# The causal mask of a forgetting-attention stage, carried by two copies of the gate row

## The chip, the cores and the metric

The kernel runs on one core of one Trainium2 chip. The metric is the device time of one execution in microseconds (us), lower is better; the kernel before takes 1213.95 us (median of 3 runs, 1213.93 to 1214.04). A core has TensorE (PE in the profile, its weight loads PEld), VectorE (DVE), ScalarE (ACT), GpSimd (POOL) and SyncE (SP), each with its own instruction stream, and 16 DMA engines that move data between HBM and on-chip memory. Transfers can be issued from SP, ACT and POOL.

## The reference: what is computed

One decoder layer on a sequence of S = 1024 rows of width D = 1024, in float32. The part that matters here is the forgetting attention (FoX): 8 heads of width 64, with a causal softmax whose scores carry the difference of two cumulative sums of log forget gates:

```python
cum = jnp.cumsum(log_f, axis=1).transpose(0, 2, 1)          # (B, heads, S)
s = jnp.einsum('bhqd,bhkd->bhqk', qi, kh) * scale
s = s + ci[..., None] - cum[:, :, None, :]
s = jnp.where(key_pos[None, :] <= q_pos[:, None], s, -jnp.inf)
p = jax.nn.softmax(s, axis=-1)
out = jnp.einsum('bhqk,bhkd->bhqd', p, vh)
```

Around it stand a retention group of 4 heads of width 128, the output projection, a layer norm, an up projection to 2 x 2816 channels with a convolution of width 3, GELU times gate, a down projection and a second layer norm.

## The kernel before

Float32 products are made of three products of split operands (high with high, high with low, low with high), so that every value has a "hi" and a "lo" tile. The kernel has four stages in time: projections and retention (a block of its own, lines 208 to 745, whose order a scheduler sets from a simulated timeline), the FoX stage (its loop stands at lines 1173 to 1226), the output projection, and the channel mixer. The change touches the end of the first block and the FoX stage.

**The FoX loop** runs over 64 steps, `s_ = 8h + i`: head h, block i of 128 queries. A step does the following.
- `fox_scores` (L783): TensorE multiplies the queries of block i with the keys 0 to 128(i+1), two products per cut (L799 with the high part of q, L800 with the low part), into a two-bank PSUM tile `ps` (two buffers). The signs are such that a masked place must become large, so TensorE then adds the mask: a bfloat16 identity times a bfloat16 triangle of 1e30 (`identb`, `maskb`, L803) into the diagonal block. DVE adds the gate row `nb` (the cumulative gates of the head, the same in all 128 partitions) and takes the minimum of each row in one pass (L805). ScalarE takes the exponential and its sum (L812), DVE the reciprocal (L815), POOL multiplies (L816).
- three steps later, `fox_turn` (L849) transposes the probabilities on TensorE (L866) and splits them: ScalarE writes the high part (L874), DVE the low part (L875). At three steps of each head `fox_pv` (L877) multiplies them with the values (L886); ScalarE copies one half of the result into `mixF` (L899), and DVE adds the other half at once (L900).
- `fox_proj` (L757) projects q and k of this head (second half of the sequence, at i < 3) and of the next one (i >= 3): 3 products of 128x512 for each of 8 pieces of the weights (L765, L766, L767). ScalarE and DVE then write `qh`, `ks`, `ql` (L771 to L781).
- `fox_w(h + 2)` at i = 4 loads the weights `wqkr` of the head after next on SP and splits them: one ScalarE copy of 128x1024 (L641), two DVE subtractions of 128x512 (L644). Each head has its own pair of weight tiles.
- `fox_alloc` (L750) at i = 3 takes the next head's tiles and loads its `nb`, 512 KB, on SP (L753), from `cum_d` in HBM. That array is written once, at the end of the first block: `cum_forget` (L709, two small products and a copy), `cum_store` (L719, a transposition, a copy, and the store L725), in the last two of 16 steps of the value projection.
- beside this, work for later stages is threaded in: the output weights are split (`park_load` L1028, `park_high` L1032, `park_low` L1039, `park_store` L1045, `wod<-park`), read back in the last head (`wo_load`, L1051), and base values for the down projection are copied in HBM (`down_base`, L1154, `td<-in_w_down_dram`, 44 copies of 256 KB at i = 6 of each head). All these issue on SP.

**Order.** Outside the first block the instructions are written in the order of the loop, and the framework moves some of them (transfers above all). Each engine then runs its stream in order and waits at semaphores. SP and ACT transfers share a set of completion semaphores, which they take in rotation. Tiles come from pools with a fixed number of 4 KB buffers (16 with tag X, 10 with tag VM); a load waits until the last reader of the buffer is done.

## Time and profile before

| what | us |
|---|---|
| median of 3 runs | 1213.95 |
| the profiled execution: its own time | 1213.8 |
| its span, first to last instruction | 1212.1 |
| TensorE busy over the span | 1195.2 |
| FoX stage in the span | 268 to 490 |
| TensorE busy in the FoX stage | 219.09 of 222 |
| one head of the FoX stage | about 25.7 |

The granted TensorE clock was 0.998 of full speed on average. A row of a timeline gives the start, the duration, engine, line, operation, output and inputs, shape and count, and, in brackets, the idle time of the engine just before it with what ended it. Matmuls are pipelined: their durations overlap, so the pace is read from the distance of their starts. A row of a group gives the count, the busy time in us, the mean of one in ns, and the idle time before. A row of the waits gives who waited for whom: us in total, times, longest us.

### The profile page before, as it was taken

What the parts mean: (1) busy time and instruction counts of PE and PEld (TensorE: products, weight loads), DVE (VectorE), ACT (ScalarE), POOL (GpSimd) and SP (SyncE); (2) the same over time, 40 slices, a digit from 0 to 9 for tenths busy, and PEclk for the clock granted to TensorE, in tenths of its full rate; (3) what the DMA queues carried; (4) which work ended last, traced back from release to release, by engine and by line L of the source; (5) the groups of instructions that cost most, each with busy time, mean ns of one, the idle gap of its engine ahead of it and who ended that gap; (6) DMA issues with size and microseconds to landing.
All of it is one profiled execution on the core that took longest, in us unless ns stands there. A gap on an engine that the chain in (4) does not pass through costs nothing.

```text
span 1212.1 us, 17100 instructions
## 1 busy us (share of the span) xinstructions
PE 1195.2 (99%) x5957; PEld 1000.4 (83%) x5957; DVE 912.2 (75%) x1749; ACT 655.7 (54%) x1209; POOL 229.6 (19%) x274
## 2 busy tenths in 40 slices
PE   8999999999999999999999999999999999999997
PEld 6788888997888888888888888888888888888885
DVE  7847657766888888456988778787787875886686
ACT  6635445346777776567754545454454555644452
POOL 0015345012333333000021322211000010000021
PEclk9999999999999999999999999999999999999999
DMA  9524354605474659223268987776554589975741
GB/s 359 227 87 121 134 158 138 202 34 175 160 239 156 191 162 356 94 79 113 87 181 203 205 210 182 176 180 175 155 139 125 145 238 289 326 247 190 263 175 70
DMA packets 94279, 216.57 MB, mean 179 GB/s; under 512 B 10784, under 2 KB 17136, under 8 KB 94192
## 3 DMA queue, kind: packets, MB, share of 16 engines
q1 hardware_dynamic: 81520, 192.40, 45.7%
q0 software_dynamic: 12672, 23.07, 11.9%
q8 instruction: 47, 0.77, 0.3%
q14 instruction: 40, 0.33, 0.1%
HBM read 173.45 MB, written 76.59 MB: 206 GB/s over the span
## 4 chain that ended last, share of the span: by engine, by line
PE 91%; DMA 4%; DVE 2%; ACT 1%; issue 0%; SPq 0%; DVEq 0%
PE rp L152 11%; PE dX L1531 10%; PE dZ L1531 7%; PE uX L1306 7%; PE uX L1307 7%; PE uX L1305 7%; PE uY L1307 5%; PE uY L1306 5%; PE uY L1305 5%; PE vp L152 4%; PE pv L886 3%; DMA ada<-in_ada_dram 3%; PE op L191 2%; PE op L189 2%; PE op L190 2%; PE pt L866 2%
## 5 line engine op out<-in xcount | busy, mean ns | idle before, releaser
L152 PE MATMUL rp<-wr,hhi 128*128 128x512 f32 x400 | 127.9, 401 | 0.0
L1517 DVE TENSOR_TENSOR dl<-dr,dh 128x1024 fp32r<-128x1024 f32 x66 | 80.5, 1238 | 33.8 <-ACT dh L1505 31.5
L816 POOL TENSOR_TENSOR S<-S,dn 128x128 f32<-128x128 f32 (+3 forms) x64 | 74.2, 1166 | 151.3 <-DVE dn L815 112.0
L1505 ACT CAST dh<-dr 128x1024 fp32r<-128x1024 f32 x58 | 59.8, 1051 | 65.6 <-DMA dr<-td 30.3
L1148 POOL DMA_DIRECT2D sd<-gd x22 | 18.1, 823 | 396.9 <-DMA sd<-y 226.2
L152 PEld LDWEIGHTS rp<-wr,hhi 128*128 128x128 f32 x400 | 71.6, 189 | 12.7
L152 PE MATMUL rp<-wr,hlo 128*128 128x512 f32 x200 | 78.6, 393 | 0.0
L1531 PE MATMUL dX<-dl,dh 128*128 128x512 f32 x176 | 68.5, 389 | 0.0
L1531 PE MATMUL dX<-dh,dl 128*128 128x512 f32 x176 | 68.5, 389 | 0.0
L1531 PE MATMUL dX<-dh 128*128 128x512 f32 x176 | 68.5, 389 | 0.0
L1320 ACT COPY u<-uX 128x512 f32<-128x512 f32 x44 | 25.8, 586 | 70.3 <-PE uX L1307 70.3
L812 ACT ACTIVATE S<-S,mn 128x128 f32<-128x128 f32 (+3 forms) x64 | 49.8, 779 | 23.9 <-DVE mn L805 23.7
L152 DVE CUSTOM_DVE_ANT_0 ada<-ada,csb,bcol 128x1024 f32<-128x1024 f32 x46 | 60.1, 1310 | 3.4 <-DMA ada<-in_ada_dram 3.3
L875 DVE TENSOR_TENSOR pt<-pt,pt 128x384 fp32r<-128x384 f32 (+3 forms) x104 | 51.9, 517 | 10.2 <-ACT pt L874 9.8
L874 ACT CAST pt<-pt 128x384 fp32r<-128x384 f32 (+3 forms) x104 | 45.2, 454 | 24.9 <-PE pt L866 23.5
L765 PE MATMUL qk<-hhi,wqh 128*128 128x512 f32 x128 | 54.3, 424 | 1.8 <-DVE ks L777 1.5
L1531 PE MATMUL dZ<-dh 128*128 128x512 f32 x132 | 51.6, 391 | 0.0
L1531 PE MATMUL dZ<-dl,dh 128*128 128x512 f32 x132 | 51.4, 389 | 0.0
L1531 PE MATMUL dZ<-dh,dl 128*128 128x512 f32 x132 | 51.4, 389 | 0.0
L767 PE MATMUL qk<-hhi,wql 128*128 128x512 f32 x128 | 51.0, 399 | 0.0
L766 PE MATMUL qk<-hlo,wqh 128*128 128x512 f32 x128 | 50.9, 397 | 0.0
L189 PE MATMUL op<-wo,mxs 128*128 128x512 f32 x128 | 50.7, 396 | 0.0
(1049 smaller groups left out, 3653.3 us busy)
## 6 DMA issues: line engine op xcount, KB each, us to landing
ada<-in_ada_dram SPq DMA_DIRECT2D x48, 512.0 KB, 3.9
td<-in_w_down_dram SPq DMA_DIRECT2D x44, 256.0 KB, 5.6
wa<-in_w_up_dram SPq DMA_DIRECT2D x22, 512.0 KB, 4.5
wb<-in_w_up_dram SPq DMA_DIRECT2D x22, 512.0 KB, 3.7
gd<-y SPq DMA_DIRECT2D x22, 512.0 KB, 2.7
sd<-y SPq DMA_DIRECT2D x44, 256.0 KB, 3.1
dr<-sd SPq DMA_DIRECT2D x44, 256.0 KB, 4.2
dr<-td SPq DMA_DIRECT2D x44, 256.0 KB, 4.4
```

The costliest lines, as they stand in the source:

```text
L152: order[key] = fn(*args, **kw)
L189: mm(pt, ahi, whi, start=start, stop=False)
L765: nc.tensor.matmul(pt, whi[:, j, :], hhi[j][:, sl], start=(j == 0), stop=False)
L767: nc.tensor.matmul(pt, wlo[:, j, :], hhi[j][:, sl], start=False, stop=(j == ND - 1))
L816: nc.gpsimd.tensor_tensor(out=Ssb[:, :span], in0=Ssb[:, :span], in1=den.to_broadcast([P, span]), op=ALU.mult,)
L875: nc.vector.tensor_tensor(out=dl, in0=src, in1=f(dh), op=ALU.subtract)
L1305: nc.tensor.matmul(pt, whi, bh, start=start, stop=False, skip_group_check=True)
L1306: nc.tensor.matmul(pt, whi, bl, start=False, stop=False, skip_group_check=True)
L1307: nc.tensor.matmul(pt, wlo, bh, start=False, stop=stop, skip_group_check=True)
L1505: nc.scalar.copy(hi, raw)
L1517: nc.vector.tensor_tensor(out=lo, in0=raw, in1=f(hi), op=ALU.subtract)
L1531: nc.tensor.matmul(pt, w_[:, 0, q], m_[:, 1, :], start=start and n_ == 0, stop=stop and n_ == 2, skip_group_check=True)
```

## The change

Line numbers of the changed kernel are given as "new L...".

- The bfloat16 mask and identity, and the product that adds them to the scores, are gone. The triangle is a float32 tile on chip.
- Each head has two copies of its gate row, `nb[0]` and `nb[1]`, loaded at i = 3 of the head before (two loads of 512 KB on SP, new L640). Two steps later, `nb_mask` adds the triangle into every second block of them: into blocks 0, 2, 4, 6 of copy 0 and 1, 3, 5, 7 of copy 1, by one accumulating transfer per copy on POOL's queue (new L645, 128 x 4 x 128).
- Step i reads copy i modulo 2, whose block i carries the mask. Behind the exponential of the step, ScalarE issues a transfer that writes block i of that copy anew from `cum_d` (new L833, 128x128, 64 KB in rows of 512 bytes), for i < 6. The minimum of step i + 2 reads that block and waits for it.
- There is one pair of weight tiles `wqh`, `wql` for all heads. The raw weights of head h + 2 are loaded at i = 6, and the split is made in four pieces of 128x256 at steps 0 to 3 of the head before, behind the last product that reads the piece of the old weights.
- The DVE additions into `mixF` are written behind the step's transpositions and their copies (new L1227) and no longer straight behind the ScalarE copy.
- The cumulative gates are made and stored two steps earlier in the value projection (steps 12 and 13), the raw weights of head 1 and the gate row of head 0 are loaded at step 14, and head 0's mask is added at step 15.

The lines between the hunks are as before; the last hunks give the calls.

```diff
 ...
     ident = cp.tile([P, P], F32, tag="ident", name="ident")
-    identb = cp.tile([P, P], BF16, tag="identb", name="identb")
-    nc.vector.tensor_copy(identb, ident)
-    maskb = cp.tile([P, P], BF16, tag="maskb", name="maskb")
-    nc.gpsimd.memset(maskb, 0.0)
+    mask = cp.tile([P, P], F32, tag="mask", name="mask")
+    nc.gpsimd.memset(mask, 0.0)
     nc.gpsimd.affine_select(
-        out=maskb, in_=maskb, pattern=[[-1, P]], compare_op=ALU.is_ge,
+        out=mask, in_=mask, pattern=[[-1, P]], compare_op=ALU.is_ge,
         fill=BIG, base=0, channel_multiplier=1,
     )
 ...
-    def fox_w(h):
-        raw = slot("R", [P, ND, P], F32, f"wqkr{h}")
-        nc.sync.dma_start(raw, w_qk[h])
-        whi = slot("X", [P, ND, P], F32R, f"wqh{h}")
-        wlo = slot("X", [P, ND, P], F32R, f"wql{h}")
-        nc.scalar.copy(whi, raw)
-        for q in range(2):
-            sl = slice(4 * q, 4 * q + 4)
-            nc.vector.tensor_tensor(
-                out=wlo[:, sl, :], in0=raw[:, sl, :], in1=f(whi[:, sl, :]), op=ALU.subtract
-            )
-        return whi, wlo
+    wraw, nbs, pins = {}, {}, {}
+
+    def nb_load(h):
+        nbs[h] = []
+        for p in range(2):
+            nb = slot("X" if h < 2 or p == 0 else "VM", [P, S], F32, f"nb{h}_{p}")
+            pins["nb"] = nc.sync.dma_start(nb, cum_rows(h, 0, S))
+            nbs[h].append(nb)
+
+    def nb_mask(h):
+        for p in range(2):
+            nc.gpsimd.dma_start(
+                nbs[h][p].rearrange("p (k t q) -> p k t q", t=2, q=P)[:, :, p, :],
+                mask.unsqueeze(1).to_broadcast([P, NT // 2, P]),
+                accum_op=ALU.add, max_dma_last_dim=2048)
+
+    def cum_rows(h, k0, k1):
+        return bass.AP(tensor=cum_d.tensor, offset=cum_d.offset + h * S + k0,
+                       ap=[[0, P], [1, k1 - k0]])
+
+    def fox_load(h):
+        wraw[h] = slot("R", [P, ND, P], F32, f"wqkr{h}")
+        nc.sync.dma_start(wraw[h], w_qk[h])
+
+    def fox_w(h, part):
+        sl = slice(2 * part, 2 * part + 2)
+        raw, (whi, wlo) = wraw[h], wqk
+        nc.scalar.copy(whi[:, sl, :], raw[:, sl, :])
+        nc.vector.tensor_tensor(
+            out=wlo[:, sl, :], in0=raw[:, sl, :], in1=f(whi[:, sl, :]), op=ALU.subtract
+        )
 ...
         if q == 3:
-            w = fox_w(0)
+            wqk = [slot("X", [P, ND, P], F32R, f"wq{n}") for n in "hl"]
+            fox_load(0)
+            for part in range(4):
+                fox_w(0, part)
         if q == 8:
             Lp = log_forget()
+        if q == 12:
+            cum = cum_forget(Lp)
+        if q == 13:
+            cum_store(cum)
         if q == 14:
-            cum = cum_forget(Lp)
-            nw = fox_w(1)
+            fox_load(1)
+            nb_load(0)
         if q == 15:
-            cum_store(cum)
+            nb_mask(0)
     blk.__exit__(None, None, None)
     mixF = {}
-    pins = {}
     def fox_alloc(h):
         t = {n: slot("X", [P, S], F32R, f"{n}{h}") for n in ("qh", "ql", "ks")}
-        t["nb"] = slot("X" if h < 2 else "VM", [P, S], F32, f"nb{h}")
-        pins["nb"] = nc.sync.dma_start(t["nb"], bass.AP(
-            tensor=cum_d.tensor, offset=cum_d.offset + h * S, ap=[[0, P], [1, S]]))
+        t["nb"] = nbs[h]
         return t
-    def fox_proj(h, w, T, t, part):
-        whi, wlo = w
+
+    def fox_proj(h, T, t, part):
+        whi, wlo = wqk
         qh, ql, ks = T["qh"], T["ql"], T["ks"]
         sl = slice(t * 512, (t + 1) * 512)
         if part == 0:
 ...
             nc.vector.tensor_copy(ql[64:, sl], f(ql[:64, sl]))
     def fox_scores(h, i, T, beside=None):
-        qh, ql, ks, nb = T["qh"], T["ql"], T["ks"], T["nb"]
+        qh, ql, ks, nb = T["qh"], T["ql"], T["ks"], T["nb"][i % 2]
         span = (i + 1) * P
         tag = "S" if i % 2 == 0 else "R" if h < FH - 1 else "VM"
         Ssb = slot(tag, [P, S], F32, f"S{h}_{i}")
 ...
         qs = slice(i * P, (i + 1) * P)
         pt = bank2(f"ps{h}_{i}")[:, off:]
         for k0, k1 in cuts:
-            last = k0 <= i * P < k1
             nc.tensor.matmul(pt[:, k0:k1], qh[:, qs], ks[:, k0:k1], start=True, stop=False)
-            nc.tensor.matmul(pt[:, k0:k1], ql[:, qs], ks[:, k0:k1],
-                             start=False, stop=not last)
-            if last:
-                nc.tensor.matmul(pt[:, i * P:(i + 1) * P], identb, maskb,
-                                 start=False, stop=True)
+            nc.tensor.matmul(pt[:, k0:k1], ql[:, qs], ks[:, k0:k1], start=False, stop=True)
         pins["min"] = nc.vector.tensor_tensor_reduce(
             out=Ssb[:, :span], in0=pt[:, :span], in1=nb[:, :span], scale=1.0, scalar=3e38,
             op0=ALU.add, op1=ALU.min, accum_out=mn,
 ...
         pins["exp"] = nc.scalar.activation(
             Ssb[:, :span], Ssb[:, :span], AF.Exp, scale=-1.0, bias=mn, accum_out=den,
         )
+        if i + 2 < NT:
+            nc.scalar.dma_start(nb[:, qs], cum_rows(h, i * P, (i + 1) * P))
         nc.vector.reciprocal(den, den)
         nc.gpsimd.tensor_tensor(
             out=Ssb[:, :span], in0=Ssb[:, :span], in1=den.to_broadcast([P, span]),
 ...
                     skip_group_check=True,
                 )
         a, b = (0, 64) if not odd else (64, 0)
+        sums = []
         for j0, j1 in ((i0, min(i1, NT // 2 - 1)), (max(i0, NT // 2), i1)):
             if j0 > j1:
                 continue
 ...
             dst = mixF[h // 4, j0 // 4][a:a + 64, (h // 2) % 2, q0:q0 + (j1 + 1 - j0) * P]
             src = pv[:, (j0 - i0) * P:(j1 + 1 - i0) * P]
             nc.scalar.copy(dst, src[b:b + 64])
-            nc.vector.tensor_tensor(out=dst, in0=src[a:a + 64], in1=dst, op=ALU.add)
+            sums.append(dict(out=dst, in0=src[a:a + 64], in1=dst, op=ALU.add))
+        return sums
     AB = cp.tile([P, 2, ND], F32, tag="AB", name="AB")
 ...
     LOADS = {0: (4, 5), 1: (6, 7), 2: (0, 1), 3: (2, 3)}
     T = {0: fox_alloc(0)}
     for part in range(4):
-        fox_proj(0, w, T[0], 0, part)
-    fox_proj(0, w, T[0], 1, 0)
+        fox_proj(0, T[0], 0, part)
+    fox_proj(0, T[0], 1, 0)
     Sb = {}
     def proj(h, i):
         if i < 3:
-            fox_proj(h, w, T[h], 1, i + 1)
+            fox_proj(h, T[h], 1, i + 1)
         elif h + 1 < FH:
-            fox_proj(h + 1, w, T[h + 1], *divmod(i - 3, 4))
+            fox_proj(h + 1, T[h + 1], *divmod(i - 3, 4))
     for s_ in range(FH * NT + LAG + 1):
         h, i = divmod(s_, NT)
 ...
                     for half in range(2):
                         mixF[h // 4, half] = slot("VM", [P, 2, 512], F32, f"mixF{h // 4}_{half}")
             if i == 3:
-                w = nw
                 if h + 1 < FH:
+                    nb_load(h + 1)
                     T[h + 1] = fox_alloc(h + 1)
             if i >= 3:
                 proj(h, i)
             k = LOWS.get(s_)
             Sb[s_] = fox_scores(h, i, T[h], None if k is None else lambda: park_low(k))
-            if i == 4 and h + 2 < FH:
-                nw = fox_w(h + 2)
             if i == 6:
                 down_base(h)
             if k is not None:
 ...
                     with tc.issue_after(pins["exp"].ins):
                         park_high(k)
         r = s_ - LAG - 1
+        sums = []
         if r >= 0 and r % NT in (2, 5, 7):
-            fox_pv(r // NT, GROUP[r % NT])
+            sums = fox_pv(r // NT, GROUP[r % NT])
         r = s_ - LAG
         if 0 <= r < FH * NT:
             fox_turn(r // NT, r % NT, Sb.pop(r))
+        for kw in sums:
+            nc.vector.tensor_tensor(**kw)
         if h < FH and not (i >= 3):
             proj(h, i)
+        if i < 4 and h + 1 < FH:
+            fox_w(h + 1, i)
+        if i == 5 and h + 1 < FH:
+            nb_mask(h + 1)
+        if i == 6 and h + 2 < FH:
+            fox_load(h + 2)
         if h == FH - 1 and i == 0:
             for q in range(2):
                 op_load(q)
```

How the rows of the engines' streams move is shown at three places of head 2. In the names the first number is the head and the second the step or the part, the last one a buffer's own number; `hhi`, `hlo` are the two parts of the modulated input, `pt` the transposed probabilities, `S` the scores after the gates, `mn` and `dn` the row minimum and the sum.

TensorE, from the scores of step 5 to the transpositions of step 2 and the projection of head 3, before:

```order
L799 MATMUL ps2_5_3981<-ks2_3561,qh2_3559 128x256
L800 MATMUL ps2_5_3981<-ks2_3561,ql2_3560 128x256
L803 LDWEIGHTS identb_71
L803 MATMUL ps2_5_3981<-maskb_77,identb_71 128x128
L866 MATMUL pt2_2_0_3995<-ident_66,S2_2_3848 128x128 x3
L765 MATMUL qk3_0_3890<-hhi6_374,wqh3_3634 128x512
```

and in the changed kernel:

```order
L820 MATMUL ps2_5_3996<-ks2_3578,qh2_3576 128x256
L821 MATMUL ps2_5_3996<-ks2_3578,ql2_3577 128x256
L885 MATMUL pt2_2_0_4010<-ident_66,S2_2_3864 128x128 x3
L787 MATMUL qk3_0_3910<-hhi6_372,wqh_2584 128x512
L788 MATMUL qk3_0_3910<-hlo6_425,wqh_2584 128x512
```

The weight load and the product with the mask are gone between the second product of the scores and the transpositions; 64 such pairs leave the stream. Behind the 64 masks stand transpositions 26 times, products of a projection 17 times, products with the values 19 times, and scores twice. The changed stream has four more places where a product follows transpositions.

ScalarE, from the exponential of step 0 on, before:

```order
L812 ACTIVATE S2_0_3762,dn2_0_3769<-S2_0_3762,mn2_0_3763 128x128
L812 ACTIVATE S2_1_3791,dn2_1_3798<-S2_1_3791,mn2_1_3792 128x256
L1032 CAST park4_0_3748<-park4_1_3749 128x512
L899 COPY mixF0_0_3186<-pv1_1_3806 64x128
L874 CAST pt1_2_0_0_3823<-pt1_6_0_3829 128x4x128
L899 COPY mixF0_1_3187<-pv1_1_3806 64x256
L874 CAST pt1_2_1_0_3825<-pt1_6_1_3836 128x3x128
L874 CAST pt1_2_0_0_3823<-pt1_7_0_3859 128x4x128
L812 ACTIVATE S2_2_3848,dn2_2_3855<-S2_2_3848,mn2_2_3849 128x384
```

and in the changed kernel:

```order
L829 ACTIVATE S2_0_3774,dn2_0_3780<-S2_0_3774,mn2_0_3775 128x128
L833 DMA nb2_0_3572<-cum_d_2396 128x128
L661 CAST wqh_2584<-wqkr3_3739 128x256
L829 ACTIVATE S2_1_3805,dn2_1_3811<-S2_1_3805,mn2_1_3806 128x256
L833 DMA nb2_1_3574<-cum_d_2396 128x128
L1053 CAST park4_0_3760<-park4_1_3761 128x512
L919 COPY mixF0_0_3188<-pv1_1_3820 64x128
L919 COPY mixF0_1_3189<-pv1_1_3820 64x256
L893 CAST pt1_2_0_0_3835<-pt1_6_0_3841 128x4x128
L893 CAST pt1_2_1_0_3837<-pt1_6_1_3848 128x3x128
L661 CAST wqh_2584<-wqkr3_3739 128x256
L893 CAST pt1_2_0_0_3835<-pt1_7_0_3875 128x4x128
```

A transfer stands behind each exponential, ahead of the copies of `park`, `mixF` and `pt`, and the weight copies of 256 columns stand between them; the ScalarE copy of 128x1024 is gone from step 4.

VectorE, from the minimum of step 6 on, with the semaphores that a row waits for (DMAHW: transfers of SP and ACT; DMASW: of POOL), before:

```order
L805 ISA S2_6_4013,mn2_6_4014<-ps2_6_4015,nb2_3562 128x896 [waits PE_49,Pool_49]
L805 ISA mn2_6_4014 128x1
L773 SCALAR_TENSOR_TENSOR ql3_3886<-qk3_0_3890,qh3_3885 64x512 [waits Activation_49]
L777 TENSOR_TENSOR ks3_3887<-qk3_0_3890,ks3_3887 64x512
L781 CAST ql3_3886<-ql3_3886 64x512 [waits DVE_49]
```

and in the changed kernel:

```order
L822 ISA S2_6_4030,mn2_6_4031<-ps2_6_4032,nb2_0_3572 128x896 [waits DMAHW2_49,PE_49,Pool_49]
L822 ISA mn2_6_4031 128x1
L795 SCALAR_TENSOR_TENSOR ql3_3908<-qk3_0_3910,qh3_3907 64x512 [waits Activation_49]
L799 TENSOR_TENSOR ks3_3909<-qk3_0_3910,ks3_3909 64x512
L803 CAST ql3_3908<-ql3_3908 64x512 [waits DVE_49]
```

The order is the same; the minimum has one more semaphore to wait for, that of the transfer that writes block 4 anew, and the three rows that make `ql` and `ks` of the next head stand behind it.

## Prediction

> **What bounds the kernel now.** I read the page's first part, then the table of the FoX stage.
>
> ```profile
> span 1212.1 us, 17100 instructions
> PE 1195.2 (99%) x5957; PEld 1000.4 (83%) x5957; DVE 912.2 (75%) x1749; ACT 655.7 (54%) x1209; POOL 229.6 (19%) x274
> ```
>
> ```profile
> 268.00:490.00 222.00, 219.09 (x1289) 184.31 (x1289) 174.44 (x478) 153.80 (x353) 74.16 (x64) 1.00 0.60 200
> ```
>
> The columns of the second are PE, weight loads, DVE, ACT, POOL, clock, DMA share and GB/s. TensorE stands still for 2.9 us in 222, at full clock, so what leaves its stream shortens the stage, and what keeps it waiting lengthens it. DVE has 47.6 us free, ACT 68.2, POOL 147.8.
>
> ```profile
> L765 PE MATMUL qk<-hhi,wqh 128*128 128x512 f32 x128 | 54.3, 424 | 1.8 <-DVE ks L777 1.5
> L803 PE MATMUL ps<-maskb,identb 128*128 128x128 bf16 x64 | 14.7, 230 | 0.0
> ```
>
> The 64 masks look like 14.7 us. That is latency in a pipeline; the price is in the starts:
>
> ```profile
> 331.96 0.34 PE L800 MATMUL ps<-ks,ql 128*128 128x384 f32 x1
> 332.14 0.23 PE L803 MATMUL ps<-maskb,identb 128*128 128x128 bf16 x1
> 332.21 1.05 PE L866 MATMUL pt<-ident,S 128*128 128x128 f32 x8
> ...
> 347.72 0.23 PE L803 MATMUL ps<-maskb,identb 128*128 128x128 bf16 x1
> 348.35 0.47 PE L765 MATMUL qk<-hhi,wqh 128*128 128x512 f32 x1 [0.39 <-DVE ks L777]
> ...
> 349.58 0.39 PE L767 MATMUL qk<-hhi,wql 128*128 128x512 f32 x1
> 349.81 0.28 PE L799 MATMUL ps<-ks,qh 128*128 128x256 f32 x1
> 349.92 0.28 PE L800 MATMUL ps<-ks,ql 128*128 128x256 f32 x1
> 350.04 0.23 PE L803 MATMUL ps<-maskb,identb 128*128 128x128 bf16 x1
> 350.08 0.48 PE L765 MATMUL qk<-hhi,wqh 128*128 128x512 f32 x1
> 350.40 0.39 PE L766 MATMUL qk<-hlo,wqh 128*128 128x512 f32 x1
> ```
>
> A product of 512 columns holds the array 0.23 us (349.58 to 349.81), one of 256 columns 0.11. A mask ahead of transpositions costs 0.07 (332.14 to 332.21). A mask ahead of a product costs 0.04, and the product behind it takes 0.32 to the next start where 0.23 is its pace: 0.13 together.
>
> The waits of the stage show who could take over:
>
> ```profile
> ACT S L812 <- DVE mn L805: 23.7, 25, 2.0
> PE qk L765 <- DVE ks L777: 1.5, 4, 0.4
> ```
>
> TensorE's largest named wait is on `ks`, 1.5 us in all, and that row stands on DVE behind the minimum of step 6.
>
> **The change part by part.** The sum goes against the profiled execution's own time, 1213.8 us: span 1212.1 and 1.7 around it. The median is 1213.95, 0.15 above.
>
> *Masks off TensorE.* By the order, 26 masks stand ahead of transpositions and 38 ahead of products: 26 x 0.07 + 38 x 0.13 = 6.8 us. Seven of them stand ahead of a product that waits for DVE anyway (as at 347.72), so 7 x 0.13 = 0.9 is not earned. Four more changes from transpositions to products, at the 0.09 by which 0.32 exceeds 0.23, take 0.4. **Gain 5.5.** Bounds: 64 x 0.04 = 2.6, if the product behind would be long anyway, and 64 x 0.13 = 8.3.
>
> *The rewrites: do they land in time?* For the tightest usual case, step 4 to step 6:
>
> ```profile
> 341.69 0.83 ACT L812 ACTIVATE S<-S,mn 128x640 f32<-128x640 f32 x1 [0.32 <-DVE mn L805]
> 342.43 0.18 ACT L812 ACTIVATION_READ_ACCUMULATOR S<-S,mn 128x1 f32 x1
> ```
>
> ```profile
> 345.78 1.09 DVE L805 CUSTOM_DVE_ANT_0 S<-ps,nb 128x896 f32<-128x896 f32 x1 [0.31 <-PE ps L803]
> 346.80 0.68 DVE L773 SCALAR_TENSOR_TENSOR ql<-qk,qh 64x512 fp32r<-64x512 f32 x1
> 347.51 0.69 DVE L777 TENSOR_TENSOR ks<-qk,ks 64x512 fp32r<-64x512 f32 x1
> ```
>
> The exponential ends at 342.52, the minimum that needs the block starts at 345.78: 3.26 us for issue and landing. No row shows a transfer on ScalarE's queue, nor one of 64 KB. The nearest are SP's, to landing:
>
> ```profile
> cum_d<-cumT SPq DMA_DIRECT2D x1, 32.0 KB, 1.8
> wod<-park SPq DMA_DIRECT2D x32, 256.0 KB, 2.3
> nb<-cum_d SPq DMA_DIRECT2D x8, 512.0 KB, 4.9
> ```
>
> and one store behind a burst of `td` copies (the answer for 352.3 to 352.6 alone):
>
> ```profile
> wod<-park SPq DMA_DIRECT2D x1, 256.0 KB, 5.1
> ```
>
> The bounds are 1.8 and 5.1. I take 2.4, a little over the 2.3 of the stores, whose size is nearest above. Then heads 1 to 6 pay nothing, with 0.9 us to spare. At 5.1 the minimum is 1.8 us late, and behind it on DVE `ql` and `ks`, and then TensorE's L765. [...]
>
> *The ends of the stage* are tighter:
>
> ```profile
> 281.40 0.29 DVE L805 CUSTOM_DVE_ANT_0 S<-ps,nb 128x128 f32<-128x128 f32 x1 [0.15 <-PE ps L803]
> ...
> 283.49 0.56 DVE L805 CUSTOM_DVE_ANT_0 S<-ps,nb 128x384 f32<-128x384 f32 x1 [0.52 <-PE ps L803]
> ...
> 469.48 1.08 DVE L805 CUSTOM_DVE_ANT_0 S<-ps,nb 128x896 f32<-128x896 f32 x1
> ```
>
> ```profile
> 281.73 0.40 ACT L812 ACTIVATE S<-S,mn 128x128 f32<-128x128 f32 x1 [2.01 <-DVE mn L805]
> ...
> 467.99 0.84 ACT L812 ACTIVATE S<-S,mn 128x640 f32<-128x640 f32 x1
> ```
>
> Head 0: the exponential of step 0 ends at 282.13, and with 2.4 the block is back at 284.5, 1.0 after 283.49. TensorE has projections to do there and the transpositions are three steps behind, so I take 0.3 (bounds 0 and 1.0). Head 7: 468.83 + 2.4 = 471.2 against 469.48, 1.7 late; products of the output projection stand between, so I take 0.7 (bounds 0 and 1.7).
>
> *The issue on ScalarE.* 48 issues at SP's price:
>
> ```profile
> 338.55 0.33 SPq L753 DMA_DIRECT2D nb<-cum_d  x1
> ```
>
> make 15.8 us in 68.2 free ones, a third of a us ahead of `park`, `mixF` and `pt` copies each time. An issue also waits for the transfer that last used its completion semaphore. In the changed order this is mostly long past, but at steps 0 and 1 of head 6 it is a `td` copy of the burst of ten just ahead, and in head 7 a `wo` load. While ScalarE stands, the copies of `pt` behind it stand, then DVE's halves, then TensorE's products with the values. No row prices it; I take 0.5 (bounds 0 and 3, three such places at about 1 us).
>
> *Gate rows and mask transfers.* The first minimum, at 281.40, now needs store, load and mask one behind another.
>
> ```profile
> 272.72 0.53 SPq L725 DMA_DIRECT2D cum_d<-cumT  x1
> ```
>
> ```profile
> sd<-sd POOLq DMA_DIRECT2D x22, 256.0 KB, 6.0
> ```
>
> The store moves up by two steps of 24 products of 256 columns at 0.11, 5.3 us, to 267.4. Plus 1.8, plus 4.9 for the load, plus 6.0 for an accumulating transfer of the same 256 KB: 280.1, hidden with 1.3 to spare; if not, its lateness comes on top of head 0's 0.3. Later heads have two steps, some 6 us, between load and mask, and as much again to the first minimum. The issue on POOL,
>
> ```profile
> L1148 POOL DMA_DIRECT2D sd<-gd x22 | 18.1, 823 | 396.9 <-DMA sd<-y 226.2 <-DMA gd<-y 170.8
> ```
>
> 0.8 us sixteen times, lies in POOL's 147.8 free us; a normalisation behind one is late by that, three steps ahead of nothing but its transpositions. The extra traffic, 8 x 512 KB, 16 x 256 KB and 48 x 64 KB, is about 11.5 MB in 222 us at 200 GB/s, a quarter more: it is hidden as long as TensorE waits for no transfer, as now; if the rewrites meet it, that is the landing time above.
>
> *The weight split.*
>
> ```profile
> L644 DVE TENSOR_TENSOR wql<-wqkr,wqh 128x512 fp32r<-128x512 f32 x12 | 7.8, 688 | 1.3 <-ACT wqh L641 0.9 <-POOL S L816 0.4
> L875 DVE TENSOR_TENSOR pt<-pt,pt 128x256 fp32r<-128x256 f32 x32 | 12.7, 411 | 0.2
> ```
>
> ```profile
> L641 ACT CAST wqh<-wqkr 128x1024 fp32r<-128x1024 f32 x6 | 6.3, 1056 | 0.4 <-DMA wqkr<-in_w_qk_dram 0.4
> L874 ACT CAST pt<-pt 128x256 fp32r<-128x256 f32 x32 | 11.2, 372 | 2.1 <-PE pt L866 1.9
> ```
>
> DVE: 4 x 0.41 for 2 x 0.69, 0.3 more a head; ACT: 4 x 0.37 for 1.06, 0.4 more. Both lie in the free time of these engines, and they leave steps 4 to 6, where DVE is on TensorE's path. The later `mixF` additions move DVE work without adding any. Zero for both; without that cover, 7 x 0.3 = 2.1.
>
> **Sum:** 1213.8 - 5.5 + 0.3 + 0.7 + 0.5 = **1209.8 us**.
>
> **The rivals.** A measurement of this kernel tells changes from about 0.2%, 2.4 us: faster is below 1211.5, slower above 1216.4.
>
> *R1, slower: the rewrites land late.* In the stage the DMA engines are 60% busy, and the rewrite is 128 rows of 512 bytes among bursts of 256 KB copies. At the 5.1 us of the store behind `td` the minimum of step 6 is 5.1 - 3.26 = 1.84 late in each of heads 1 to 6, and since TensorE waits for `ks` already (348.35), it comes through: 6 x 1.84 = 11.0, so 1220.8. It decides from a landing of about 3.9 on, where 6 x 0.66 eats the 4.0 gained. For it: the 5.1. Against it: those stores stand in SP's queue behind the very copies, and the median store lands in 2.3. [...] 0.2.
>
> *R2, no change: the masks were nearly free.* If the weight load of the next product sets the 0.32, the masks hide in it and only 0.04 each comes back: 2.6 - 1.5 = 1.1, so 1212.7. For it: weight loads take 184 of 222 us. Against it: 349.58 to 349.92 runs three products with three loads at full pace. ScalarE held at semaphores at its bound of 3 gives the same verdict with the full 5.5: 1213.8 - 5.5 + 0.3 + 0.7 + 3 = 1212.3. 0.28.
>
> *R3, faster still: the waits go too.* The split out of step 4 and the later additions free DVE ahead of `ks`, and half of TensorE's 2.9 idle us goes as well, with no loss at the ends: 1213.8 - 5.5 - 1.4 = 1206.9. Against it: that wait hangs on the scores of step 6 (345.78 waits for PE) and one minimum, not on the weight split. 0.1.
>
> **How the numbers follow.** My forecast has 0.42; with R3 that makes faster 0.52; same 0.28 (R2); slower 0.20 (R1). The range reaches from a little below R3, 1206.5, to 1218, which takes R1 up to landings of 4.6. The forecast's own range is 1207.5 to 1211.5.
>
> **What would show it.** Right: L765 starts at the pace of 0.23 behind the 256-wide scores; the rewrites land within 3 us; DVE's minima wait for no DMA in heads 1 to 6. TensorE's idle time in the stage stays within 2.5 to 4.5 us, and the stage is about 4 us shorter. Wrong: minima of steps 5 and 6 that wait for `nb<-cum_d`, with L765 waiting for `ks` by as much (R1); a 512-wide product that still takes 0.32 behind scores (R2); ScalarE idle ahead of the rewrite's line by more than a few us in all.

## The result, and the profile after

The changed kernel takes 1247.5 us (median of 4 runs, 1243.29 to 1251.54) against 1213.95: 33.5 us slower, ratio 1.0276 with a 95% interval of 1.0236 to 1.0315. The forecast was 1209.8, its range ended at 1218. The profiled execution took 1243.29, 29.5 above the profiled one of before. Two executions in a far slower state, one of e5 below (1805.57 us at a granted clock of 0.62) and one of the kernel before (4277.38 us), stand in no comparison.

The first part of the page of the changed kernel, and the queues of its third part (packets, MB, share of 16 engines):

```profile
span 1241.6 us, 17160 instructions
PE 1200.4 (97%) x5893; PEld 1004.7 (81%) x5893; DVE 915.9 (74%) x1764; ACT 660.1 (53%) x1233; POOL 253.1 (20%) x290
...
q0 software_dynamic: 21120, 27.27, 14.3%
q10 hardware_dynamic: 6912, 3.15, 1.1%
```

TensorE has 64 matmuls less and is busy 5.2 us longer. Queue q10 is new: ScalarE's rewrites have a queue of their own, 6912 packets. POOL's q0 has 8448 packets more, the mask transfers. Where the time went, by the same stretch of the table of busy times as in the prediction:

```profile
268.00:490.00 222.00, 196.78 (x1085) 166.10 (x1084) 164.94 (x449) 144.20 (x343) 89.07 (x75) 0.96 0.76 216
```

TensorE stands still for 25.2 us where it stood for 2.9, at a granted clock of 0.96 where it was 1.00, and the DMA engines are busy 76% for 60%. The last minimum of head 7 starts at 504.45 where it started at 475.22, so 29.2 of the 29.5 us lie ahead of it. The waits of the stage (us in total, times, longest), 268 to 520 us:

```profile
POOL nb L645 <- DMA nb<-cum_d: 25.3, 4, 20.8
DVE S L822 <- DMA nb<-cum_d: 19.1, 10, 4.5
PE qk L787 <- DVE ks L799: 15.1, 7, 4.9
```

The minimum waits for transfers into `nb`, 19.1 us, and TensorE's projection for `ks`, 15.1 for 1.5 before: the chain that the prediction described under R1. (20.8 us of the first row lie ahead of the first mask, while POOL waits for the first gate row.) One instance, in head 1: ScalarE issues the rewrite of block 4 as the exponential of step 4 starts, SP a burst of four `td` copies around it, and the minimum of step 6 starts when the block is back.

```profile
324.16 0.83 ACT L829 ACTIVATE S<-S,mn 128x640 f32<-128x640 f32 x1 [0.40 <-DVE mn L822]
324.16 0.33 ACTq L833 DMA_DIRECT2D nb<-cum_d  x1
```

```profile
323.39 4.00 SPq L1175 DMA_DIRECT2D td<-in_w_down_dram  x4
```

```profile
nb<-cum_d ACTq DMA_DIRECT2D x1, 64.0 KB, 6.2
```

```profile
330.55 1.09 DVE L822 CUSTOM_DVE_ANT_0 S<-ps,nb 128x896 f32<-128x896 f32 x1 [2.75 <-DMA nb<-cum_d]
331.56 0.08 DVE L822 DVE_READ_ACCUMULATOR2_ANT mn<- 128x1 f32 x1
331.56 0.68 DVE L795 SCALAR_TENSOR_TENSOR ql<-qk,qh 64x512 fp32r<-64x512 f32 x1
332.27 0.69 DVE L799 TENSOR_TENSOR ks<-qk,ks 64x512 fp32r<-64x512 f32 x1
```

```profile
329.75 0.40 PE L821 MATMUL ps<-ks,ql 128*128 128x512 f32 x1
333.11 0.77 PE L787 MATMUL qk<-hhi,wqh 128*128 128x512 f32 x1 [2.97 <-DVE ks L799]
333.68 0.63 PE L788 MATMUL qk<-hlo,wqh 128*128 128x512 f32 x1
334.11 0.63 PE L789 MATMUL qk<-hhi,wql 128*128 128x512 f32 x1
334.53 0.63 PE L787 MATMUL qk<-hhi,wqh 128*128 128x512 f32 x1
```

The rewrite lands 6.2 us after its issue, at 330.4. The minimum follows 0.16 later, `ql` and `ks` behind it, and TensorE has stood for 2.97 us. The last rows show a cost that the prediction had nowhere: behind the wait, products of 512 columns start every 0.43 us where they started every 0.23. The table of busy times says why. In the stretch of the wait the granted clock is 1.00, in the next one of 3.41 us it is 0.50 (the columns are those of the table above, the clock is the third number from the end):

```profile
329.58:332.99 3.41, 0.57 (x3) 0.13 (x1) 2.41 (x5) 1.29 (x3) 2.82 (x3) 1.00 0.99 252
332.99:336.40 3.41, 3.29 (x9) 2.64 (x10) 3.21 (x9) 0.97 (x3) 1.68 (x1) 0.50 1.16 302
```

In this trace 20.5 us of the FoX stage run at half clock, in that of before none. TensorE is busy for 16.9 of them, work that would take about half as long at 0.23 us a product instead of 0.43. By this estimate some 8 of the 29.5 us are lost to the clock, on top of the waits themselves.

How long the transfers take to land in the stage (median; of the 48 rewrites, the landing of 35 is in the trace):

```profile
td<-in_w_down_dram SPq DMA_DIRECT2D x44, 256.0 KB, 6.7
nb<-mask POOLq DMA_DIRECT2D x16, 256.0 KB, 8.2
nb<-cum_d ACTq DMA_DIRECT2D x48, 64.0 KB, 5.2
```

### The profile page after: what moved, and what is told of

It is laid out like the page before. It is cut to its first block, busy times and chain, and to the rows that moved or that the text cites. A ratio compares the mean times of both kernels' runs of the same rounds, so it can differ in the third digit from the quotient of the medians.

```text
span 1241.6 us, 17160 instructions
## 1 busy us (share of the span) xinstructions
PE 1200.4 (97%) x5893; PEld 1004.7 (81%) x5893; DVE 915.9 (74%) x1764; ACT 660.1 (53%) x1233; POOL 253.1 (20%) x290
## 3 DMA queue, kind: packets, MB, share of 16 engines
q10 hardware_dynamic: 6912, 3.15, 1.1%
## 4 chain that ended last, share of the span: by engine, by line
PE 87%; DVE 5%; DMA 4%; ACT 2%; issue 1%; SPq 0%; ACTq 0%; POOL 0%; DVEq 0%; POOLq 0%
PE rp L150 11%; PE dX L1559 10%; PE dZ L1559 7%; PE uX L1334 6%; PE uX L1333 6%; PE uX L1335 6%; PE uY L1333 5%; PE uY L1335 5%; PE uY L1334 5%; PE vp L150 4%; PE op L187 2%; PE op L189 2%; PE op L188 2%; DMA nb<-cum_d 2%; PE pv L905 2%; PE fa L150 2%
## 5 line engine op out<-in xcount | busy, mean ns | idle before, releaser
L835 POOL TENSOR_TENSOR S<-S,dn 128x128 f32<-128x128 f32 (+3 forms) x64 | 80.4, 1320 | 85.0 <-DVE dn L834 73.8
L822 DVE CUSTOM_DVE_ANT_0 S<-ps,nb 128x128 f32<-128x128 f32 (+3 forms) x64 | 48.1, 752 | 34.5 <-DMA nb<-cum_d 19.1
L787 PE MATMUL qk<-hhi,wqh 128*128 128x512 f32 x128 | 55.1, 430 | 15.1 <-DVE ks L799 15.1
```

What stands on the lines that cost most here:

```text
L787: nc.tensor.matmul(pt, whi[:, j, :], hhi[j][:, sl], start=(j == 0), stop=False)
L835: nc.gpsimd.tensor_tensor(out=Ssb[:, :span], in0=Ssb[:, :span], in1=den.to_broadcast([P, span]), op=ALU.mult,)
```

## The experiments

Three theories were open: **A**, the rewrites land too late (R1); **B**, the mask transfers do it, through POOL and through their own landing; **C**, the rest of the change (one weight pair, its split in four pieces, later loads and additions) costs time. Differences are taken to the kernel before as it ran in the same group: 1214.49, 1214.20 and 1214.29 us. "e9" and the like are the runs' labels, shortened.

### e1: both small transfers become engine work

```diff
-            nc.gpsimd.dma_start(<blocks of parity p>, mask..., accum_op=ALU.add, ...)
+            nc.gpsimd.tensor_tensor(out=blocks_, in0=blocks_, in1=mask..., op=ALU.add)
...
-            nc.scalar.dma_start(nb[:, qs], cum_rows(h, i * P, (i + 1) * P))
+            nc.scalar.copy(nb[:, qs], T["nb"][1 - i % 2][:, qs])
```

> The changed kernel, with both kinds of small transfer replaced by engine work: POOL adds the triangle into the copies (128 x 4 x 128, two additions a head), and block i is written anew by a ScalarE copy from the other copy of the gate row, where that block carries no mask. If the whole loss comes from transfers that land late or hold an engine (both theories below say so), the stage runs as my sum had it: 1208 to 1211 us. If the loss comes from the rest of the change (one weight pair, split in four pieces, later additions, moved loads), it stays well above 1220.

Measured: 1219.24 us, 4.75 above before (ratio 1.0038, 1.0023 to 1.0053). The two kinds of transfer, put into engine work, make 28.3 us of the loss (1247.5 to 1219.24). But what is left still loses, so both readings of the expectation are half right: theory C has a part.

### e2: only the masks by POOL

The first hunk of e1 alone.

> The changed kernel with the triangle added by POOL itself; the rewrites stay transfers on ScalarE's queue. Theory A (the rewrites land about 5 us after their issue in the bursts, later than the minimum two steps on allows): most of the loss stays, 1230 to 1245. Theory B (the mask transfers do it: one at a time on POOL's queue, they hold the normalisations behind them and land 5 to 12 us late): the loss goes, 1210 to 1218.

Measured: 1237.71, 23.2 above before (1.0191, 1.0168 to 1.0214). With the rewrites alone as transfers 18.5 us of the 28.3 are there (1237.7 - 1219.2). Theory A holds; B has the smaller part.

### e3: only the rewrites by ScalarE

The second hunk of e1 alone.

> The changed kernel with block i written anew by a ScalarE copy; the masks stay transfers on POOL's queue. Theory A (late rewrites): the loss goes but for the start of head 0, 1210 to 1218. Theory B (mask transfers hold POOL): most of the loss stays, 1230 to 1245. If the two need each other (512-byte packets of the one make the other late), both this and the former lie in between.

Measured: 1231.74, 17.3 above (1.0145, 1.0128 to 1.0162). It lies between the expectations of A and B: the mask transfers alone cost 12.5 us (1231.7 - 1219.2). 18.5 and 12.5 make 31.0 against 28.3 together, so neither needs the other. What the mask transfers do is seen on POOL and TensorE in head 3 of e3:

```profile
375.92 1.31 POOL L645 DMA_DIRECT2D nb<-mask  x1 [4.69 <-DVE mn L822]
376.74 1.57 POOL L835 TENSOR_TENSOR S<-S,dn 128x512 f32<-128x512 f32 x1
385.71 1.31 POOL L645 DMA_DIRECT2D nb<-mask  x1 [7.39 <-DMA td<-in_w_down_dram]
386.52 4.82 POOL L835 TENSOR_TENSOR S<-S,dn 128x640 f32<-128x640 f32 x3
```

```profile
nb<-mask POOLq DMA_DIRECT2D x1, 256.0 KB, 9.5
```

```profile
388.35 1.33 PE L885 MATMUL pt<-ident,S 128*128 128x128 f32 x5 [4.35 <-POOL S L835]
```

The first transfer takes 9.5 us and lands at 385.4; the second is issued 0.3 later, though the trace names a transfer that had long landed as its releaser. Three normalisations stand behind it, and TensorE's transpositions wait for them 4.35 us. In the trace of the changed kernel, 8 of the 15 later mask transfers are issued 0.26 to 0.58 us after the landing of the one before, and none ahead of it. Head 0, where loads and masks follow one another, loses 4.9 us in e3 between the first minima of heads 0 and 1, 23.58 against 18.65 in e1. The same place in the changed kernel: the mask of the second copy lands at 287.60, and the minimum of step 1 has waited for it.

```profile
287.71 0.42 DVE L822 CUSTOM_DVE_ANT_0 S<-ps,nb 128x256 f32<-128x256 f32 x1 [4.44 <-issue]
```

### e12: the masks in long rows

Based on e3. The row of zeros and triangles is laid down in HBM once, and each mask transfer adds 128 rows of 4 KB from it instead of 512 pieces of 512 bytes.

```diff
-            nc.gpsimd.dma_start(<blocks of parity p>, mask..., accum_op=ALU.add, ...)
+            nc.gpsimd.dma_start(nbs[h][p], wide[:, P - p * P:P - p * P + S], accum_op=ALU.add)
```

> The run with blocks written anew by ScalarE and masks as transfers (1231.7), with each mask transfer in rows of 4 KB: zeros and triangles of a whole row from HBM, 512 KB in 128 rows instead of 256 KB in 512 pieces. Theory B: POOL's queue holds about one transfer of 512 pieces, and the next one, with POOL behind it, stands until the first has landed. With 128 rows two transfers go out behind each other at once, POOL's normalisations come free, and the time falls to 1220 to 1226. If every accumulating transfer waits for the one before whatever its pieces: 1230 to 1236, each issued 0.3 us after the landing before.

Measured: 1229.43 (2 runs; 1.0125, 1.0103 to 1.0147), 2.3 below e3. The issue rows of POOL, first of the changed kernel and then of e12:

```profile
273.84 1.49 POOL L645 DMA_DIRECT2D nb<-mask  x1 [20.78 <-DMA nb<-cum_d]
282.98 1.31 POOL L645 DMA_DIRECT2D nb<-mask  x1 [7.66 <-PE qk L788]
```

```profile
273.23 1.06 POOL L651 DMA_DIRECT2D nb<-wide  x1 [20.77 <-DMA nb<-cum_d]
276.62 0.87 POOL L651 DMA_DIRECT2D nb<-wide  x1 [2.32 <-DMA nb<-cum_d]
278.52 0.87 POOL L651 DMA_DIRECT2D nb<-wide  x1 [1.03 <-DMA nb<-cum_d]
```

```profile
nb<-wide POOLq DMA_DIRECT2D x16, 512.0 KB, 8.5
```

In this form the second is issued 3.4 us after the first and the third 1.9 after the second, at a median landing of 8.5 us, so here an accumulating transfer did not wait for the one before: that part of theory B stands. That the number of pieces decides is not shown alone, since the source (a row in HBM for a tile on chip) and the bytes changed with it. And the time hardly falls. The transfers land as late as before (8.5 us), POOL still stands where a mask transfer waits for its gate row to land, and 13.7 us of the stage run at half clock against 6.8 in e3. Which of these carries the remaining 10 us (1229.4 against e1) is not settled.

### e8: without the bursts

Based on e2, with all 44 `td` copies issued behind the FoX stage. They delay the next stage, so the total of 1245.83 (one run) says nothing; only the FoX stage is read. A hunk that is not shown ties these copies to the loads of `x`.

```diff
-            if i == 6:
-                down_base(h)
...
             op_split(0, 0)
+            for m in range(FH):
+                down_base(m)
```

> The changed kernel with the triangle added by POOL, rewrites as transfers, and the 44 copies td moved behind the FoX stage, where their 11 MB delay the next stage: only the FoX stage is read. If the bursts make the rewrites late, they land in 2.8 to 3.2 us everywhere, TensorE's gaps at the projections fall from 2 to 3 us to under 0.8, and the stage is 15 us shorter than with bursts. If the rewrites collide with loads and stores of any kind, landings of 5 us and the gaps stay.

Median landing of the rewrites in the stage, e2 and then e8 (35 and 38 of the 48 landings are in the traces):

```profile
nb<-cum_d ACTq DMA_DIRECT2D x48, 64.0 KB, 4.1
```

```profile
nb<-cum_d ACTq DMA_DIRECT2D x48, 64.0 KB, 3.1
```

The shortest landing is 2.8 us, in e8 as in the two others. From the first minimum of head 1 to that of head 7, e8 takes 157.9 us, e2 166.1, e1 159.8: in these heads the bursts cost 8.2 us. But the expected sign was missed. TensorE's projections still wait 8.8 us for `ks` in e8, 2.8 at the longest, where 11.7 and 3.1 stand in e2 and gaps below 0.8 were expected (268 to 500 us). What went with the bursts is in good part the clock; the same stretch in e2 and then in e8:

```profile
304.06:470.12 166.06, 152.12 (x854) 130.16 (x853) 135.64 (x357) 116.31 (x274) 73.33 (x60) 0.97 0.63 199
```

```profile
301.79:459.66 157.87, 147.77 (x854) 126.07 (x853) 134.95 (x358) 116.85 (x274) 73.26 (x60) 1.00 0.46 147
```

In e2, 10.2 us of it ran at half clock, in e8 none; an estimate as above puts this at 5 of the 8.2 us. No run has e1 without the bursts, so that e8 is faster here than e1 does not show that the rewrites are free without them. The expectation of 15 us less was too much also because heads 0 and 7 stay slow: from the first to the last minimum of head 7 e8 takes 26.6, e2 26.0 and e1 20.0. There the `wo` loads are under way, and the rewrites land after 6 to 8 us. At step 4 of heads 3 and 5 of e8, some 3 us behind the issue of a gate-row load, they still land after 4.3.

### e4: only the mask product away

```diff
-            nc.tensor.matmul(pt[:, k0:k1], ql[:, qs], ks[:, k0:k1], start=False, stop=not last)
-            if last:
-                nc.tensor.matmul(pt[:, i * P:(i + 1) * P], identb, maskb, start=False, stop=True)
+            nc.tensor.matmul(pt[:, k0:k1], ql[:, qs], ks[:, k0:k1], start=False, stop=True)
```

> The kernel before without the product that adds the mask (the causal mask is left out, nothing else is changed): the price of the masks on TensorE alone. My terms without the four extra changes to transpositions: 6.8 - 0.9 = 5.9 less, 1208.0. If the masks were nearly free (R2, 0.04 each): 1211.4. If the product behind each is all slowed by them (64 x 0.13): 1205.7.

Measured: 1211.84 against 1214.49, ratio 0.9979 (0.9970 to 0.9988): 2.65 us, not 5.9. The price of one mask on TensorE is as I had it: behind scores of 256 columns a projection now starts after 0.12 and the next one after 0.23.

```profile
349.87 0.28 PE L800 MATMUL ps<-ks,ql 128*128 128x256 f32 x1
349.99 0.40 PE L765 MATMUL qk<-hhi,wqh 128*128 128x512 f32 x1
350.22 0.40 PE L766 MATMUL qk<-hlo,wqh 128*128 128x512 f32 x1
```

The rest went into waits:

```profile
268.00:490.00 222.00, 216.62 (x1238) 184.25 (x1238) 176.62 (x480) 154.93 (x355) 74.06 (x64) 1.00 0.60 200
```

```profile
L765 PE MATMUL qk<-hhi,wqh 128*128 128x512 f32 x128 | 53.6, 419 | 3.6 <-DVE ks L777 3.6
```

TensorE's idle time in the stage grew from 2.9 to 5.4 us, of which the wait for `ks` alone from 1.5 to 3.6. 2.65 earned and 2.5 waited make 5.2 of the 5.9; the rest is not followed.

### e5: only the rest

The change without its masks: the mask stays on TensorE, one gate row for each head, no small transfers; one weight pair, the pieces, the later additions and loads as in the change.

> The kernel before with only the rest of the change: one weight pair split in four pieces, raw weights loaded at step 6, later additions into mixF, moved cumulative gates. The mask stays on TensorE, one copy of the gate row, no small transfers. Theory C (this rest costs the 7 us by which the first run, 1219.2, stands above the kernel without the mask product, 1211.8): 1219 to 1222. If the rest is free, as my sum had it, and ScalarE's and POOL's new copies and additions cost the 7 us: 1213 to 1215.

Measured: 1217.90 (median of 5 runs), ratio 1.0033 (1.0020 to 1.0045), 3.7 us above by the medians and 4.0 by the ratio. That lies between the two expectations: a part that I had put at zero costs about 4 of the 7 us, so theory C has the larger share. Where the other 3 come from, this run does not say; e9 below, which keeps the new copies and additions, stands only 1.0 above e4. Which part of the rest costs the time is read from the next three runs.

### e6: additions into mixF at once

Based on e1.

```diff
-            sums.append(dict(out=dst, in0=src[a:a + 64], in1=dst, op=ALU.add))
+            nc.vector.tensor_tensor(out=dst, in0=src[a:a + 64], in1=dst, op=ALU.add)
```

> The first run's kernel (masks added by POOL, blocks written anew by ScalarE) with the additions into mixF straight behind the ScalarE copy again. Theory C1: the later addition keeps the PSUM buffer of the values' product, and TensorE's transpositions wait for it (gaps of 0.6 to 1.2 us at six places of the first run, 4.5 us in all): 1214 to 1215.5, and no L885 that waits for L1227. If the gaps have another cause: 1219.

Measured: 1219.68 (1.0044, 1.0029 to 1.0059), no different from e1's 1219.24. The gaps of TensorE ahead of its transpositions stay (1.09 us at 306.68, 0.98 there in e1) and wait for the DVE halves of `pt` instead. Theory C1 falls: the late additions stood ahead of the gap and did not cause it.

### e7: raw weights at step 4

Based on e6.

```diff
-        if i == 6 and h + 2 < FH:
+        if i == 4 and h + 2 < FH:
             fox_load(h + 2)
```

> The former kernel with the raw weights of the head after next loaded at step 4 again instead of step 6. Theory C2: at step 6 the load lands after ScalarE reaches its first piece (it stood 2.0 us in head 1 of the first run, and TensorE's products with the values 1.4): 1.5 to 2.5 us less than the former, 1212 to 1213.5. If the lateness is hidden but in that one place: within 1 us of the former.

Measured: 1217.83 (1.0028, 1.0018 to 1.0038), 1.85 less. The saving is as theory C2 has it; the total stays above its figure, since e6 had not fallen. The clock may be part of it: the traces of e1 and e6 have 3.4 us at half clock some 3 to 4 us behind this wait, that of e7 has none. What had stood, in e1:

```profile
327.69 0.41 ACT L661 CAST wqh<-wqkr 128x256 fp32r<-128x256 f32 x1 [2.03 <-DMA wqkr<-in_w_qk_dram]
328.00 1.14 ACT L829 ACTIVATE S<-S,mn 128x1024 f32<-128x1024 f32 x1
```

The piece of the next weights (its copy, new L661) stands ahead of an exponential on ScalarE and holds it until its load has landed.

### e9: the pieces one step later

Based on e7.

```diff
-        if i < 4 and h + 1 < FH:
-            fox_w(h + 1, i)
+        if 1 <= i < 5 and h + 1 < FH:
+            fox_w(h + 1, i - 1)
```

> The kernel of the run with early weights, with the four pieces of the weight split at steps 1 to 4 instead of 0 to 3. Theory C3: the piece of step 0 meets POOL's multiplication of 1024 columns in all heads but the first, and DVE is held until that ends (1.07 to 1.47 us for 0.41 alone), which makes the minimum of step 1 and then a transposition late (gaps of 1.1 us in four heads): 1213 to 1215, no piece above 0.5 us beside such a multiplication. If the gaps come from more copies and additions on ScalarE and POOL: 1217 to 1218.5 as before.

Measured: 1212.86 (10 runs, 1212.00 to 1214.41), ratio 0.9988 (0.9978 to 0.9998): 5.0 less than e7, and 1.4 below the kernel before. It is the one version of this study that keeps the mask and is faster than before, by about a tenth of a per cent. Head 2 of e7, DVE and POOL, from the piece of step 0 to the minimum of step 1:

```profile
328.84 1.47 DVE L662 TENSOR_TENSOR wql<-wqkr,wqh 128x256 fp32r<-128x256 f32 x1
330.22 0.41 DVE L822 CUSTOM_DVE_ANT_0 S<-ps,nb 128x256 f32<-128x256 f32 x1
```

```profile
328.12 2.43 POOL L835 TENSOR_TENSOR S<-S,dn 128x1024 f32<-128x1024 f32 x2 [2.78 <-PE ps L821]
```

and DVE in e9:

```profile
327.98 0.42 DVE L822 CUSTOM_DVE_ANT_0 S<-ps,nb 128x256 f32<-128x256 f32 x1
328.61 0.83 DVE L662 TENSOR_TENSOR wql<-wqkr,wqh 128x256 fp32r<-128x256 f32 x1
```

The minimum of step 1 starts 1.7 us behind that of step 0 (at 326.29), where it was 3.1 in e7 (at 327.15). In heads 1 to 6 it is 1.7 to 2.2 in e9 and 3.0 to 3.2 in e7. TensorE's transpositions wait less for DVE by as much as the time falls; 268 to 490 us, e7 and then e9:

```profile
PE pt L885 <- DVE pt L894: 5.8, 9, 1.2
```

```profile
PE pt L885 <- DVE pt L894: 0.7, 3, 0.2
```

The expectation missed in one point: the pieces are still longer than 0.41 us beside POOL's multiplications (0.60 to 0.84 at step 1 in five heads, about 1.04 at the last piece in four), and their mean is 582 ns against 596 in e7. So the long pieces themselves did not go. What went is the minimum of step 1 standing behind a piece of 1.07 to 1.47 us. ScalarE's copies of the pieces moved by a step as well; that they had no part in it is not shown alone.

### e10 and e11: the minimum of step 6 behind ks

e10 is based on e9, e11 on the kernel before; in both, DVE's minimum of step 6 is ordered behind `ks`.

```diff
+        if i == 6 and h + 1 < FH:
+            with tc.issue_after(pins["ks"].ins):
+                least()
```

> The former kernel with the minimum of step 6 ordered behind the rows on DVE that make ql and ks of the next head. Theory D: without its masks TensorE only runs earlier into the wait for ks (0.65 us a head in the kernel without the mask product), because the minimum of step 6 stands ahead of ks: these waits go, 2 to 4 us less than the former run, 1210 to 1212. If ks is bound by ScalarE's copies and not by the minimum: within 1 us of the former.

> The kernel before, masks on TensorE, with only the minimum of step 6 ordered behind ks. Theory D: its 1.5 us of waits for ks go, 1212.5 to 1213.5. If the later minimum costs as much elsewhere (the exponential of step 6, the transpositions three steps on): 1214 to 1216.

Measured: 1214.33 (1.0003, 0.9993 to 1.0012) and 1214.04 (0.9998, 0.9988 to 1.0008). Theory D falls: nothing is gained on the kernel before, and e9 loses its 1.4. In e10 the wait for `ks` shrinks only from 2.2 to 1.6 us and the waits of the values' product for `pt` grow from 2.3 to 2.8. It seems that the wait moves with what DVE does first.

## Why the prediction was wrong

**The sum of the loss.** From 1247.5 to e9's 1212.86: both kinds of transfer 28.3 (rewrites 15.8 to 18.5, masks 9.8 to 12.5, by whether the other is still there; some of both is half clock behind the waits), the raw weights' load 1.9, the order of the pieces 5.0, the later additions -0.4. That leaves 1.0 above the kernel without any mask, e4.

**"I take 2.4 ... Then heads 1 to 6 pay nothing."** This is the step that failed most, a term of the sum that was mis-sized: the rewrites took 5.2 in the median, 2.8 at the least and 8.4 at the most (35 of 48). The mechanism and the point from which it decides were R1's, and the row that was right was the one I set aside: the store behind the `td` burst, 5.1. I argued that it stood in SP's own queue behind the copies, while a rewrite would not. q10 shows that the rewrites do have their own queue, and that it did not keep them clear of the bursts: with the bursts moved away the median landing falls from 4.1 to 3.1 us (e2 and e8). Not even the shortest landing, 2.8 us, came down to the 2.4. R1 at 1220.8 was too low as well: step 4's landing was 5.7 to 8.4 in four of the heads, the ends of the stage lost 6 us in head 7 alone (26.0 in e2 against 20.0 in e1), where I had 0.7, and behind most of the longest waits TensorE ran at half clock, a term that stood nowhere in the sum.

**The mask transfers, "hidden with 1.3 to spare".** I had priced the issue (0.8 us) and the landing (6.0). The trace shows 1.3 for the issue and 8.2 for the landing, and in e3 POOL stands for up to 7.4 us ahead of the next one. "A normalisation behind one is late by that" was the right place with the wrong number: what stood behind it waited for a landing, not for an issue. At the start, the store went out at 267.3, as I had it, but the first mask took 8.9 and not 6.0, so that it landed at 282.72 for a minimum due at 281.40. The mask of the second copy, which the sum did not have at all, had to follow it and landed at 287.60. The masks cost 9.8 to 12.5 us.

**The weight split, "zero for both", with a bound of 2.1.** e7 and e9 together put 6.8 us on it. I counted engine time (0.3 and 0.4 us a head) and looked at the free time of whole engines. What decided was the order: a piece ahead of the minimum of step 1 on DVE, 1.07 to 1.47 us long beside POOL's multiplications in e7, and a piece ahead of an exponential on ScalarE that waits for a load moved two steps nearer to its use. The later additions were free, as I had them.

**"Gain 5.5."** The price of a mask on TensorE was right: 2.65 us earned and 2.5 more waited in e4. The step that failed is "seven of them stand ahead of a product that waits for DVE anyway, 0.9 is not earned". With every mask that it was spared ahead of it, not just with the last one, TensorE only came earlier to the same wait, for `ks`, which grew from 1.5 to 3.6 us. The idle row ahead of L765 names DVE: there DVE's pace was the bound, though TensorE was busy for 99%.

**The issue on ScalarE, 0.5**, is not seen: the rewrite goes out no later than 0.2 us behind the start of the step's exponential, but for one that is 1.1 behind. At step 4 that is 0.8 us earlier than I assumed. That the rewrites were late in spite of this says how far the 2.4 was off.

**The chances.** R1 with 0.2 was too low for a price that rested on the choice between two rows of the same kind, one of them with the same burst as here.

## What to carry to other kernels

A transfer that an instruction two steps on waits for has to be priced by the slowest row near its size under the traffic that it will meet, not by the median (here 5.1 and 2.3, and 5.2 was measured); if the same bytes lie on chip, a copy of 0.28 us on an engine with free time does what a transfer of 2.8 to 8.4 us did. When work is put on an in-order engine, price what then stands behind it, not its busy time: the 0.4 us pieces cost 5 us more where they stood than one step later. Work taken from an engine that is 99% busy is earned only up to the next wait of that engine (2.65 of 5.9 us in e4). And a wait of that engine can cost more than its length, if its clock falls behind it (it was 0.50 behind the wait of 2.97 us in head 1; some 8 us in all by the estimate above).

## What the runs showed of the hardware that I had not expected

- In the trace of the changed kernel the granted clock is 0.50 in five stretches of the FoX stage, four of 3.41 us and one, the fourth, of 6.83, and 1.00 in the rest of it. TensorE's products of 512 columns start every 0.43 us in them instead of every 0.23. They begin at 302.26, 332.99, 363.70, 391.01 and 496.82, which lie 9, 9, 8 and 31 times 3.413 us apart, each beside a wait of TensorE (3.27, 2.97, 2.73, 4.93 and 2.20 us) that ends from 1.1 us ahead of that start to 2.6 behind it. In slices of 3.413 us laid from 302.26 both ways, the stage has six in which TensorE was busy for 1.3 us or less (0.35, 0.58, 1.14, 1.11, 0.79 and 1.30), and all six are followed by half clock. One wait of 2.27 us, ending at 450.27, lies across the border of two slices at 449.04; TensorE is busy for 2.28 and 2.18 us of them, and full clock follows. The busy time alone does not decide: in e2 a slice with 1.8 us is followed by half clock and one with 1.5 is not. What else does, no run shows. This kernel's runs spread over 8 us where those of before spread over 0.1 to 1.4; the two shorter of its four runs had a mean clock of 0.990 and 0.991, the two longer 0.985.
- In the traces of the changed kernel and of e3, POOL never issues an accumulating transfer of 512 pieces before the one before has landed; 15 of the 30 later ones, with all that stands behind them on POOL, are issued 0.26 to 0.58 us after that landing. With 128 rows of 4 KB from HBM (e12) the next ones went out 3.4 and 1.9 us after the one before, at a median landing of 8.5.
- DVE's subtraction of two on-chip operands, 0.41 us in the median of 24 in the changed kernel (300 to 480 us), took 1.07 to 1.47 in six of six heads of e7 where POOL's multiplication of 1024 columns had begun before it. Why they take longer there no run shows.
